# PEER on one Trainium2 core: 192 of 512 tokens by gathered rows instead of 128, the odd 64 tokens in column halves

## The chip, the cores and the metric

The kernel runs on one core of one Trainium2 chip. The metric is the device time of one execution in microseconds (us). The program has five engines' instruction streams: PE (TensorE, matrix products), DVE (VectorE), ACT (ScalarE), POOL (GpSimd) and SP (SyncE, which here only issues transfers). Transfers from ACT, SP and POOL go through queues of their own to the core's 16 DMA engines.

## The reference, cut to what matters

The program is one layer of a trunk over 512 tokens of width 1024: two mixers, their merge, and then the PEER feed-forward part, the only one that the change touches. All of it is float32.

```python
def peer_ffn(x, w_q, sub_keys, u, v):              # 8 heads, top 16 each, 128 x 128 experts
    def block(xb):
        q = (xb @ w_q).reshape(TB, H, 2, PEER_HALF)
        s = jnp.einsum('thpc,phnc->thpn', q, sub_keys)
        s1, i1 = lax.top_k(s[:, :, 0], K)
        s2, i2 = lax.top_k(s[:, :, 1], K)
        ...
        top_s, pos = lax.top_k(cand, K)
        eidx = jnp.take_along_axis(cidx, pos, axis=-1).reshape(TB, H * K)
        g = jax.nn.softmax(top_s, axis=-1).reshape(TB, H * K)
        h = jnp.einsum('tkd,td->tk', u[eidx], xb)
        a = jax.nn.gelu(h, approximate=False) * g
        return jnp.einsum('tk,tkd->td', a, v[eidx])
    ...
x = x + peer_ffn(rmsnorm(x, norm_ffn), ...)
return rmsnorm(x, norm_final)
```

Each token picks 128 of 16384 experts; u and v hold one row of 1024 float32 an expert, 64 MiB each.

## The kernel before

**Two ways to the same sum.** The first block of 128 tokens is done *by rows*: for each of its 128 picks k, one indirect transfer on POOL's queue (`row`, L757) fetches 128 rows of 4 KB, one a token, from u or v, and one DVE instruction uses them: `u_row` (L762) multiplies by the token and sums, `v_row` (L770, L772) adds a weighted row to `acc`. That makes 256 gathers of 512 KB. The other three blocks (384 tokens) are done *densely*: u and v are read whole, in 128 chunks j of 128 experts; `u_chunk` (L739) forms all 384 x 128 products and the gelu, and `v_parts` and `v_product` (L883, L911) multiply by a matrix of weights, which is zero for experts that were not picked, and by the chunk of v.

**Products in three passes.** A float32 operand is cut into a rounded high part (ACT, type fp32r) and the rest, the low part (DVE, L110, L895, L908). `mm3` (L74) then issues three PE products, lines 77, 78 and 79. Products that PE takes in float32 itself (L148 and L652, for example) appear in the profile as two records each.

**Stages.** Four stages follow each other from 456 us on:

1. The *picks*: for each of 8 heads two `query` products of 512 columns, `scores`, three `u_chunk`s (seven in the last head), then `picks` (L670), a long run of DVE instructions that ends in `eidx` (L709), the row numbers.
2. The *weights*: 48 `u_chunk`s (j from 28 to 75), and between them the dense weight matrix G, made eight tokens at a time (`g_group`, L834, 48 groups: two DVE instructions, 16 PE products, two ACT copies) and written to memory, `g_d`, in 12 transfers of 2 MB. The gelu results of the first 76 chunks go to memory too (`h_d`).
3. *u and v together*: 52 steps, each with one `u_chunk` (j from 76 on) and one chunk of v.
4. *v alone*: the chunks of v whose gelu results lie in `h_d`, 76 in all, then the sums, the final norm and the output.

`some_rows` (L777) sets how many rows are placed at each chunk: the rates R0 to R3 for the four stages are 0, 1, 2.9 and 0.95, and none is placed at the last NOROW = 8 chunks of stage 2. `pace[0]`, the last low part on DVE, is the point behind which the rows are placed. The row buffers (`gp`, L749) are four: a gather waits until DVE has used the row four before it.

## Time and profile before

| | |
|---|---|
| median of 3 runs | 1708.71 us (1706.27 to 1711.08) |
| the profiled execution | 1711.65 us, its span 1709.9 us |
| PE busy | 1675.5 us, 98% of the span |
| PE weight loads busy | 1465.9 us, 86% |
| DVE, ACT, POOL busy | 1340.8, 729.3, 377.0 us |
| moved by DMA | 414.90 MB, 243 GB/s over the span |
| mean granted clock of TensorE | 0.996 |

Times are of one profiled execution. Busy time of PE is modelled at the ends of products, which overlap; the distance between the starts of two products tells the pace. DMA share is the mean busy share of the 16 DMA engines; it can read a little over 1.00 where packets overlap.

### The profile page before, as it was taken

The numbers are of one execution on the slowest core, as the hardware profiler recorded it, in microseconds if no ns is written. First come the engines' busy times: TensorE is split into PE (matmuls) and PEld (weight loads), VectorE is DVE, ScalarE is ACT, GpSimd is POOL, SyncE is SP. The second block draws the span as 40 slices with busy tenths as digits, with TensorE's granted clock in tenths as the row PEclk, the third lists the DMA queues.
The fourth block names the chain that finished last, engine by engine and source line by source line (L and its number), as shares of the span: only waits on it lengthen the run. The fifth ranks groups of instructions, "written<-read, shape, count | busy, mean of one in ns | idle before, by whom it ended". The sixth has DMA issues, their size and how long they took to land.

```text
span 1709.9 us, 24687 instructions
## 1 busy us (share of the span) xinstructions
PE 1675.5 (98%) x9095; PEld 1465.9 (86%) x9097; DVE 1340.8 (78%) x2573; ACT 729.3 (43%) x1052; POOL 377.0 (22%) x284
## 2 busy tenths in 40 slices
PE   8999999999999999999999999999999999999997
PEld 6988887777798888999999999999999978888886
DVE  4776887547699999998988588878887888877785
ACT  4322226734443434566666433333333333333333
POOL 2000000000010000232322144444444442333320
PEclk9999999999999999999999999999999999999999
DMA  7321233127454334798988899999999999999983
GB/s 234 131 81 50 75 125 116 56 94 241 163 177 128 126 123 131 248 359 316 359 316 336 278 338 335 337 331 319 322 317 344 324 336 353 357 333 346 321 299 131
DMA packets 172472, 414.90 MB, mean 243 GB/s; under 512 B 14744, under 2 KB 85784, under 8 KB 170688
## 3 DMA queue, kind: packets, MB, share of 16 engines
q10 hardware_dynamic: 101072, 141.70, 24.4%
q1 hardware_dynamic: 34416, 137.40, 22.6%
q0 software_dynamic: 36864, 134.23, 22.4%
q8 instruction: 71, 1.16, 0.3%
q14 instruction: 49, 0.40, 0.1%
HBM read 366.86 MB, written 49.04 MB: 243 GB/s over the span
## 4 chain that ended last, share of the span: by engine, by line
PE 41%; issue 33%; DMA 11%; POOL 9%; DVE 5%; ACT 1%; POOLq 0%; SPq 0%; ACTq 0%; DVEq 0%
POOL row L757 8%; PE acc L79 6%; PE acc L77 6%; PE acc L78 6%; DMA row<-in_peer_u,eidx 5%; PE ps_mm L77 5%; PE ps_mm L79 5%; PE ps_mm L78 5%; DMA row<-in_peer_v,eidx 4%; PE ps_hg L379 2%; PE ps_hg L77 1%; PE ps_yb L460 1%; PE ps_hg L78 1%; PE ps_hg L79 1%; DMA v_raw<-in_peer_v 1%
## 5 line engine op out<-in xcount | busy, mean ns | idle before, releaser
L108 ACT CAST w_hi<-w_raw 128x1024 fp32r<-128x1024 f32 (+2 forms) x215 | 219.2, 1020 | 401.0 <-PE ps_u L78 125.4
L110 DVE TENSOR_TENSOR w_lo<-w_raw,w_hi 128x1024 fp32r<-128x1024 f32 (+2 forms) x215 | 254.9, 1185 | 84.4 <-ACT w_hi L108 72.1
L757 POOL DMA_INDIRECT row<-in_peer_u,eidx x128 | 178.5, 1394 | 553.6 <-DVE hh L762 503.6
L77 PE MATMUL ps_u<-xfH,w_hi 128*128 128x384 f32 x800 | 274.0, 343 | 1.4 <-ACT hg L744 1.4
L78 PE MATMUL ps_u<-xfL,w_hi 128*128 128x384 f32 x800 | 270.6, 338 | 0.0
L79 PE MATMUL ps_u<-xfH,w_lo 128*128 128x384 f32 x800 | 269.9, 337 | 0.0
L757 POOL DMA_INDIRECT row<-in_peer_v,eidx x128 | 178.6, 1395 | 275.5 <-DVE acc L772 253.3
L78 PE MATMUL acc<-v_lo,aH 128*128 128x512 f32 x540 | 211.2, 391 | 3.3 <-DVE v_lo L895 3.3
L77 PE MATMUL acc<-v_hi,aH 128*128 128x512 f32 x540 | 212.1, 393 | 1.4 <-ACT aH L906 1.1
L79 PE MATMUL acc<-v_hi,aL 128*128 128x512 f32 x540 | 212.1, 393 | 0.1
L906 ACT CAST aH<-aj 128x384 fp32r<-128x384 f32 x128 | 65.6, 513 | 308.7 <-DVE aj L903 138.1
L772 DVE SCALAR_TENSOR_TENSOR acc<-row,ah,acc 128x1024 f32<-128x1024 f32 x127 | 162.6, 1281 | 21.4 <-DMA row<-in_peer_v,eidx 20.7
L762 DVE CUSTOM_DVE_ANT_0 scr<-row,xf 128x1024 f32<-128x1024 f32 x128 | 156.3, 1221 | 20.1 <-DMA row<-in_peer_u,eidx 19.3
L77 PEld LDWEIGHTS ps_u<-xfH,w_hi 128*128 128x128 f32 x800 | 150.2, 188 | 3.5 <-ACT hg L744 1.7
L78 PEld LDWEIGHTS ps_u<-xfL,w_hi 128*128 128x128 f32 x800 | 150.5, 188 | 2.2
L79 PEld LDWEIGHTS ps_u<-xfH,w_lo 128*128 128x128 f32 x800 | 150.2, 188 | 0.0
L895 DVE TENSOR_TENSOR v_lo<-v_raw,v_hi 128x1024 fp32r<-128x1024 f32 x90 | 110.0, 1223 | 24.1 <-ACT v_hi L894 23.5
L78 PEld LDWEIGHTS acc<-v_lo,aH 128*128 128x128 f32 x540 | 101.7, 188 | 24.0 <-DVE v_lo L895 3.6
L79 PEld LDWEIGHTS acc<-v_hi,aL 128*128 128x128 f32 x540 | 101.8, 188 | 23.2 <-DVE aL L908 0.8
L77 PEld LDWEIGHTS acc<-v_hi,aH 128*128 128x128 f32 x540 | 101.7, 188 | 22.1 <-ACT aH L906 1.4
L894 ACT CAST v_hi<-v_raw 128x1024 fp32r<-128x1024 f32 x90 | 94.4, 1048 | 51.6 <-PE acc L79 19.9
L858 ACT COPY stg<-ps_g 128x512 f32<-128x512 f32 x96 | 99.6, 1158 | 3.3 <-PE ps_g L855 3.3
(313 smaller groups left out, 3367.4 us busy)
## 6 DMA issues: line engine op xcount, KB each, us to landing
w_raw<-in_uT SPq DMA_DIRECT2D x128, 512.0 KB
v_raw<-in_peer_v ACTq DMA_DIRECT2D x90, 512.0 KB
g_d<-stg SPq DMA_DIRECT2D x12, 2048.0 KB
gj<-g_d ACTq DMA_DIRECT2D x32, 768.0 KB
w_raw<-in_peer_v ACTq DMA_DIRECT2D x38, 512.0 KB
w_raw<-in_wT SPq DMA_DIRECT2D x31, 512.0 KB
h_d<-hg ACTq DMA_DIRECT2D x76, 192.0 KB
hgr<-h_d ACTq DMA_DIRECT2D x76, 192.0 KB
```

The lines of the kernel that those rows point to most:

```text
L77: pe.matmul(ps, lh, rh, start=first, stop=False, **kw)
L78: pe.matmul(ps, lh, rl, start=False, stop=False, **kw)
L79: pe.matmul(ps, ll, rh, start=False, stop=last, **kw)
L108: act.copy(hi[:, :n], raw[:, :n])
L110: pace[0] = dve.tensor_tensor(lo[:, :n], raw[:, :n], hi[:, :n].bitcast(F32), op=OP.subtract)
L757: pool.indirect_dma_start(out=g, out_offset=None, in_=A[tab], in_offset=bass.IndirectOffsetOnAxis(ap=eidx[:, k:k + 1], axis=0))
L762: dve.tensor_tensor_reduce(out=scr, in0=row("peer_u", k), in1=xf0, scale=1.0, scalar=0.0, op0=OP.mult, op1=OP.add, accum_out=hh[:, k:k + 1])
L772: dve.scalar_tensor_tensor(acc, row("peer_v", k), ah[:, k:k + 1], acc, op0=OP.mult, op1=OP.add)
L858: act.copy(stg[:, :, t4:t4 + 4].rearrange("p j t -> p t j"), ps)
L894: act.copy(vh, raw)
L895: pace[0] = dve.tensor_tensor(vl, raw, vh.bitcast(F32), op=OP.subtract)
L906: act.copy(aH, gj)
```

## The change

- **Tokens.** The rows take 192 tokens. The odd 64 (the first half of block 1) share one set of 64 gathers: partitions 0 to 63 fetch the picks 0 to 63 and partitions 64 to 127 the picks 64 to 127 of the same tokens (`eidh`, `gwh`, `xfh`). So there are 64 more gathers for u and 64 more for v, 384 in all. The dense part has NT = 320 tokens: `u_chunk` products have 320 columns instead of 384, G has 40 groups and 10 transfers instead of 48 and 12, `h_d` rows are 1280 B instead of 1536 B.
- **The odd half block in v.** Dense block 1 is now 64 tokens. It meets v in float32 products with 64 columns of weights (`v_halves`), once for two chunks: the even chunk's product goes to partitions 0 to 63 of `hacc`, the odd one's to 64 to 127. At the end a product with the matrix `sel` adds the halves, of `hacc` and of the row sums.
- **Plain chunks.** Each third chunk of v (42 of 128) is multiplied in float32 (L946 of the new file), one product in place of three, and its high and low parts are not made.
- **Low parts on POOL.** In the picks, `query` and `u_chunk` make the low part with a POOL instruction instead of a DVE instruction: 16 and 28 of them.
- **Rates.** R0 to R3 are 1.4, 1, 3.4 and 1.75, NOROW is 6. `pace[0]` is `eidx` in the picks, and the weighting instruction of a plain chunk.
- Buffers: chunks of v have four raw buffers of their own; `o_sum` is dropped, the sum is formed in `x2`; `gfin` is loaded at the start of stage 3.

```diff
-    def weight(src, n=1024, q=None):
+    def weight(src, n=1024, q=None, cut=None):
...
-        pace[0] = dve.tensor_tensor(lo[:, :n], raw[:, :n], hi[:, :n].bitcast(F32), op=OP.subtract)
+        i = (cut or dve).tensor_tensor(lo[:, :n], raw[:, :n], hi[:, :n].bitcast(F32), op=OP.subtract)
+        if cut is None:
+            pace[0] = i
...
+    HT = P // 2
+    T0 = P + HT
+    NT = S - T0
-    NT = 3 * P
...
-        hi, lo = cut(weight(A["peer_wq"][m]), 8)
+        hi, lo = cut(weight(A["peer_wq"][m], cut=pool), 8)
...
-    R0, R1, R2, R3, NOROW = 0, 1, 2.9, 0.95, 8
+    R0, R1, R2, R3, NOROW = 1.4, 1, 3.4, 1.75, 6
+    PLAIN = 3
...
-            mm3(ps[:, :NT], (hi[:, c, :], lo[:, c, :]), (xfH[:, c, P:], xfL[:, c, P:]), c == 0, c == 7)
+            mm3(ps[:, :NT], (hi[:, c, :], lo[:, c, :]), (xfH[:, c, T0:], xfL[:, c, T0:]), c == 0, c == 7)
...
-    rows = list(range(P))
+    rows = [(0, k) for k in range(P)] + [(1, k) for k in range(HT)]
...
-            u_chunk(j, psum([P, 512], "hg"))
+            u_chunk(j, psum([P, 512], "hg"), pool)
...
-            some_rows(R0, h * 16)
+            some_rows(R0, h)
...
-        work = [(b, t0) for b in range(3) for t0 in range(0, P, TB)]
+        work = [(b, t0) for b in range(3) for t0 in range(0 if b else HT, P, TB)]
...
+    hacc = [vp.tile([P, 512], F32, name="hacc_%d" % n) for n in range(2)]
...
+    def v_product(b, n, part, first, last):
+        gj, raw, a, v = part
+        ns = slice(n * 512, (n + 1) * 512)
+        bs = slice(b * P, (b + 1) * P)
+        if a is None:
+            pe.matmul(accs[b][n], gj[:, HT:][:, bs], raw[:, ns], start=first, stop=last)
+        else:
+            mm3(accs[b][n], (a[0][:, bs], a[1][:, bs]), (v[0][:, ns], v[1][:, ns]), first, last)
+
+    def v_halves(pair, first, last):
+        for n in range(2):
+            for z, (gj, raw, _, _) in enumerate(pair):
+                pe.matmul(hacc[n][z * HT:(z + 1) * HT, :], gj[:, :HT], raw[:, n * 512:(n + 1) * 512], start=first, stop=last)
...
-    vrows = list(range(P))
+    vrows = [(1, k) for k in range(HT)] + [(0, k) for k in range(P)]
...
+        return v_parts(j, ahead.pop(0) if ahead else None, q % PLAIN == PLAIN - 1)
+
+    for q in range(0, P - 2, 2):
+        pair = []
+        for i in range(2):
+            part = chunk(q + i)
+            pair.append(part)
+            for b in range(2):
+                for n in range(2):
+                    v_product(b, n, part, q + i == 0, False)
+            some_rows(R2 if q < P - LEAD else R3)
+        v_halves(pair, q == 0, False)
```

The order of the instructions moves at three places.

PE in stage 4, one chunk of v. Before, the three products repeat for two halves of the width (`acc_0`, `acc_1`) and three blocks, 18 in all; the first block:

```order
L77 MATMUL acc_0_9386<-w_hi,aH 128x512
L78 MATMUL acc_0_9386<-w_lo,aH 128x512
L79 MATMUL acc_0_9386<-w_hi,aL 128x512
L77 MATMUL acc_1_9387<-w_hi,aH 128x512
L78 MATMUL acc_1_9387<-w_lo,aH 128x512
L79 MATMUL acc_1_9387<-w_hi,aL 128x512
```

Now, the column halves of a finished pair, then a plain chunk (L946), then a chunk in three passes:

```order
L953 MATMUL hacc_9317<-v_raw,aj 64x512 x2
L953 MATMUL hacc_9318<-v_raw,aj 64x512 x2
L946 MATMUL acc_0_9313<-v_raw,aj 128x512
L946 MATMUL acc_1_9314<-v_raw,aj 128x512
L946 MATMUL acc_0_9315<-v_raw,aj 128x512
L946 MATMUL acc_1_9316<-v_raw,aj 128x512
L77 MATMUL acc_0_9313<-w_hi,aH 128x512
L78 MATMUL acc_0_9313<-w_lo,aH 128x512
L79 MATMUL acc_0_9313<-w_hi,aL 128x512
```

Two blocks are left of three, and four products of 64 columns come once a pair, so that the array changes between 128 and 64 columns twice a pair.

POOL from the feed-forward norm to the end. Before, only the small norm steps and the gathers:

```order
L71 TENSOR_TENSOR rs_r<-rs_ms,half 128x4 x3
L71 TENSOR_TENSOR rs_r<-rs_ms,half 128x1 x4
L757 DMA row<-in_peer_u,eidx 128x1024 x128
L757 DMA row<-in_peer_v,eidx 128x1024 x128
L71 TENSOR_TENSOR rs_r<-rs_ms,half 128x1 x4
```

Now the low parts (L110) and the gathers (L773) stand in one line; the first heads:

```order
L110 TENSOR_TENSOR w_lo<-w_raw,w_hi 128x1024 x6
L773 DMA row<-in_peer_u,eidx 128x1024 x2
L110 TENSOR_TENSOR w_lo<-w_raw,w_hi 128x1024
L773 DMA row<-in_peer_u,eidx 128x1024 x2
L110 TENSOR_TENSOR w_lo<-w_raw,w_hi 128x1024
L773 DMA row<-in_peer_u,eidx 128x1024 x3
L110 TENSOR_TENSOR w_lo<-w_raw,w_hi 128x1024
```

39 gathers stand ahead of the last of the 44 low parts, and a low part behind a gather waits until the gather may be issued.

DVE at the end of one head's picks. Before, low parts stand between the steps:

```order
L110 TENSOR_TENSOR w_lo<-w_raw,w_hi 128x1024
L705 TENSOR_TENSOR oh<-oh 128x8x128
L705 TENSOR_TENSOR oh<-oh 128x8x64
L705 TENSOR_TENSOR oh<-oh 128x8x32
L707 TENSOR_TENSOR e_4599<-oh 128x128
L709 SCALAR_TENSOR_TENSOR eidx<-e_4599 128x16
L110 TENSOR_TENSOR w_lo<-w_raw,w_hi 128x1024
```

Now the rows' multiply-and-sum (L779, two instructions a row) stands there instead:

```order
L715 TENSOR_TENSOR oh<-oh 128x8x32
L717 TENSOR_TENSOR e_4614<-oh 128x128
L719 SCALAR_TENSOR_TENSOR eidx<-e_4614 128x2x16
L779 ISA scr,hh<-row,xf_3281 128x1024
L779 ISA hh 128x1
L670 MAX v_4817<-sc 128x8
```

Three to five of them stand behind each head's `eidx`.

## Rows read from the trace of the kernel before

**Rows 1.** The page, part 2: DMA share in tenths in 40 slices of the span, and GB/s.
```profile
DMA  7321233127454334798988899999999999999983
GB/s 234 131 81 50 75 125 116 56 94 241 163 177 128 126 123 131 248 359 316 359 316 336 278 338 335 337 331 319 322 317 344 324 336 353 357 333 346 321 299 131
```
**Rows 2.** Windows, the four stages: stretch, its length, PE, PEld, DVE, ACT, POOL busy, PEclk, DMA share, GB/s.
```profile
456.00:691.00 235.00, 227.82 (x1250) 206.53 (x1248) 218.51 (x945) 100.40 (x148) 5.58 (x7) 1.00 0.42 136
691.00:955.00 264.00, 261.05 (x1988) 252.84 (x1989) 220.85 (x238) 170.55 (x207) 71.05 (x45) 1.00 0.88 322
955.00:1380.00 425.00, 420.54 (x2110) 381.56 (x2108) 341.62 (x434) 148.08 (x204) 192.06 (x142) 1.00 0.93 325
1380.00:1697.00 317.00, 316.75 (x1368) 257.93 (x1369) 247.96 (x304) 112.33 (x158) 90.06 (x66) 0.99 0.92 319
```
**Rows 3.** The timeline of PE: a stretch of stage 4, first and last of 53 products.
```profile
1499.81 0.39 PE L79 MATMUL acc<-w_hi,aL 128*128 128x512 f32 x1
...
1511.81 0.39 PE L77 MATMUL acc<-v_hi,aH 128*128 128x512 f32 x1
```
**Rows 4.** The timeline of PE: one u chunk of stage 3, 24 products of 384 columns.
```profile
1104.93 0.34 PE L77 MATMUL ps_u<-xfH,w_hi 128*128 128x384 f32 x1
...
1109.15 0.39 PE L77 MATMUL acc<-v_hi,aH 128*128 128x512 f32 x1
```
**Rows 5.** The timeline of PE: 20 products of 256 columns in the first query.
```profile
468.82 0.28 PE L78 MATMUL ps_mm<-xfL,w_hi 128*128 128x256 f32 x1
...
471.13 1.05 PE L652 MATMUL ps_tr<-kT,qT 128*128 128x128 f32 x8
```
**Rows 6.** The timeline of PE: four float32 products of 512 columns, eight records.
```profile
12.20 4.00 PE L148 MATMUL ps_tr<-sq,ones 128*128 128x512 f32 x8 [1.24 <-ACT sq L147]
15.63 0.70 PE L77 MATMUL ps_mm<-w_hi,xnH 128*128 128x290 f32 x1
```
**Rows 7.** The timeline of PE: the 16 products of one group of G.
```profile
701.84 1.10 PE L855 MATMUL ps_g<-ow,oz 128*128 128x128 f16 x16
```
**Rows 8.** Groups by shape, DVE: line, operation, count, busy us, mean ns, idle before.
```profile
L110 DVE TENSOR_TENSOR w_lo<-w_raw,w_hi 128x1024 fp32r<-128x1024 f32 x191 | 233.1, 1220 | 80.8 <-ACT w_hi L108 68.6 <-PE ps_g L855 10.5 <-issue 1.5
L772 DVE SCALAR_TENSOR_TENSOR acc<-row,ah,acc 128x1024 f32<-128x1024 f32 x127 | 162.6, 1281 | 21.4 <-DMA row<-in_peer_v,eidx 20.7
L762 DVE CUSTOM_DVE_ANT_0 scr<-row,xf 128x1024 f32<-128x1024 f32 x128 | 156.3, 1221 | 20.1 <-DMA row<-in_peer_u,eidx 19.3
L895 DVE TENSOR_TENSOR v_lo<-v_raw,v_hi 128x1024 fp32r<-128x1024 f32 x90 | 110.0, 1223 | 24.1 <-ACT v_hi L894 23.5 <-issue 0.4
```
**Rows 9.** Windows of the gathers alone (L757), POOL busy and count by stage.
```profile
456.00:691.00 235.00, 4.49 (x5) 1.00 0.42 136
691.00:955.00 264.00, 71.05 (x45) 1.00 0.88 322
955.00:1380.00 425.00, 192.06 (x142) 1.00 0.93 325
1380.00:1697.00 317.00, 89.49 (x65) 0.99 0.92 319
```
**Rows 10.** The page, part 3: the queue of the gathers.
```profile
q0 software_dynamic: 36864, 134.23, 22.4%
```
**Rows 11.** Windows of 100, 20 and 4 us with the highest DMA rates.
```profile
1400.00:1500.00 100.00, 99.92 (x434) 81.17 (x433) 85.07 (x104) 37.95 (x52) 30.47 (x25) 1.00 1.01 356
1420.00:1440.00 20.00, 20.00 (x89) 16.31 (x88) 16.03 (x20) 7.22 (x10) 4.99 (x5) 1.00 1.06 368
824.00:828.00 4.00, 4.00 (x28) 4.00 (x26) 3.70 (x5) 2.67 (x4) 0.57 (x1) 1.00 1.09 465
```
**Rows 12.** Groups by shape: PE's first 64-row product after 128-row ones, and the next.
```profile
L77 PE MATMUL ps_hg<-akH,aqH 64*128 64x512 f32 x6 | 3.0, 494 | 0.3 <-issue 0.3
L78 PE MATMUL ps_hg<-akL,aqH 64*128 64x512 f32 x6 | 2.3, 391 | 0.0
```
**Rows 13.** Groups by shape, POOL: its only wide elementwise step.
```profile
L145 POOL TENSOR_TENSOR sq<-xt 128x512 f32<-128x512 f32 x4 | 5.3, 1324 | 8.5 <-DMA xt<-in_xT 8.4
```

More of the change, by code (lines that the diff above doesn't have):

```diff
@@ L593, in norm_ffn @@
         dve.scalar_tensor_tensor(xf, x2[:, b, :], r, gffn, op0=OP.mult, op1=OP.mult)
+        if b == 1:
+            for z in range(2):
+                act.dma_start(xfh[z * HT:(z + 1) * HT, :], xf[:HT, :])
         for c4 in range(2):
@@ L768, in v_row, with u_row @@
-    def v_row(k):
+    def u_row(half, k):
+        c = half * P + k
+        dve.tensor_tensor_reduce(out=scr, in0=row("peer_u", half, k), in1=xfh if half else xf0, scale=1.0, scalar=0.0,
+                                 op0=OP.mult, op1=OP.add, accum_out=hh[:, c:c + 1])
+        n = HT if half else P
+        if k == n - 1:
+            cs = slice(half * P, half * P + n)
+            act.activation(ah[:, cs], hh[:, cs], AF.Gelu)
+            dve.tensor_tensor(ah[:, cs], ah[:, cs], gwh if half else gw0[:, 0, :], op=OP.mult)
@@ L775, in trunk, with some_rows @@
+    rows = [(0, k) for k in range(P)] + [(1, k) for k in range(HT)]
     due = [0]
-    def some_rows(rate, avail=P):
+    def some_rows(rate, heads=9):
         due[0] += rate
@@ L946, in last_rows, with chunk @@
         finish(0)
-    for q, j in enumerate(order[:-2]):
+    def chunk(q):
+        j = order[q]
         if LEAD + AHEAD + q < P:
             ahead.append(u_chunk(LEAD + AHEAD + q, up.tile([P, 512], F32, name="ps_u")))
-        a, v = v_parts(j, ahead.pop(0) if ahead else None)
-        for b in range(3):
-            for n in range(2):
-                v_product(b, n, a, v, q == 0, False)
-        some_rows(R2 if q < P - LEAD else R3)
-        if q == P - 6:
-            last_rows()
-    if 0 not in fin:
-        last_rows()
```

177 lines of the change are left out of this document (98 added, 79 removed).

## The prediction

> **What bounds the kernel now.** I read the page's slices first, then the windows of the stages, then PE's timeline inside a stage, then the groups by shape. The slices show two halves of a program: up to slice 17 the DMA engines have room, from then on they are nine tenths busy until the last slice but one [rows 1]. The windows tell the four stages apart [rows 2]: the picks take 235 us, the weights 264, u and v together 425, v alone 317; 456 us lie ahead of them and 13 behind. PE is busy for 97 to 100% of each, at a granted clock of 0.99 to 1.00 (the 2.4 GHz level), and the timeline says that this is no artefact of modelled ends: in stage 4, 53 products of 512 columns start one behind the other in 12.00 us, 0.231 us each [rows 3], and a u chunk of 24 products of 384 columns takes 4.22 us, 0.176 each [rows 4]. A step of stage 3 is then 4.22 + 18 x 0.231 = 8.38 us by PE, and 52 of them 436 us, against the 425 of the window, which holds 51. So before the change PE's pace sets stages 3 and 4. DMA is the next limit and close: share 0.93 and 0.92 over the two stages, 325 and 319 GB/s, and in one stretch of 100 us 1.01 at 356 GB/s [rows 2, 11]. In the picks DVE is at 93% and PE at 97%; there DMA idles (0.42).
>
> That is what the change trades: PE work goes away, and DMA work comes in at the stages where DMA has 7% left.
>
> **PE's side.** The dense u products get narrower. 256 columns take 2.31 / 20 = 0.1155 us a product [rows 5], 384 take 0.176; 320 are not in the trace, the middle is 0.146. That gives back 24 x 0.030 = 0.72 us a chunk: 20 us in the picks (28 chunks), 35 in stage 2 (48), 37 in stage 3 (52). Eight groups of G fewer give 8 x 1.1 = 9 us in stage 2 [rows 7].
>
> The v products: a float32 product of 512 columns is two records; eight records start 3.43 us ahead of the next product, 0.43 each, so 0.86 us a product [rows 6]. A chunk cost 18 x 0.231 = 4.16 us. A chunk in three passes now costs 12 x 0.231 = 2.77, a plain one 4 x 0.86 = 3.44: 86 x 2.77 + 42 x 3.44 = 383 us. The column halves are four float32 products a pair, 64 pairs. No row has such a product. From above: they run one after the other, 3.44 us a pair, 220 us in all. From below: the even and the odd one run wholly side by side, 110 us. I take 138: each is two records in order, and only the second record of the one and the first of the other are in different columns, so that eight records fill five times 0.43. With 52 narrower u chunks (52 x 3.50 = 182) stages 3 and 4 need 383 + 182 + 138 = 703 us of PE (675 to 785), against 52 x 4.22 + 128 x 4.16 = 752 before, in 742 us of windows, which again hold one chunk less.
>
> Twice a pair the array goes from 128 columns to 64 or back. The nearest row is the change from 128 rows to 64: the first such product takes 494 ns where the next takes 391 [rows 12], 0.10 us, so 128 changes cost about 13 us, and PE stands at 716. The Trainium skill (TensorEngine Tiling (Array Packing), Key Properties) says that a change of tiling mode drains the engine, which speaks against this change, and that different tiles can load and multiply in parallel, which speaks for it; the row shows a cost of the first kind, and no row of this trace shows the second. By a whole drain, an estimate of one product's tail (0.39 - 0.23 us [rows 3]), the 13 us would be 20.
>
> **DMA's side.** A gather moves 0.524 MB; by its queue's row 256 of them hold 22.4% of the engines' span, 1.50 us each [rows 10]. There are 128 more. Of all gathers 5 lay in the picks, 45 in stage 2, 207 behind it [rows 9] (one is counted twice). By the new order 39 lie in the picks and 42 in stage 2, so 303 behind: 96 more, +50.3 MB. Less is read of G (10 blocks for 12, -4.2 MB) and of `h_d` (76 x 32 KiB, -2.5 MB). Stages 3 and 4 moved 425 x 325 + 317 x 319 = 239.2 MB; now 282.8. At which rate? From below 322 GB/s, what they had; from above 368, the best 20 us of stage 4 [rows 11]. I take 353, just under the 356 of the full 100 us, since there the engines were at 1.01 and PE was not held up: 282.8 / 353 = **801 us**, against PE's 716. So DMA becomes the limit of stages 3 and 4, and they go from 742 to 801 us: **+59**. PE then waits about a tenth of the time, in pieces, and its products cost nothing more.
>
> **The other engines there.** DVE gets 96 rows at 1.22 + 0.08 or 1.28 us (+124 us) and loses 42 low parts of v (-51) and some of the narrower steps [rows 8]: 590 + 60 of 801 us, less full than before. POOL issues a gather in about 1.4 us, 303 x 1.4 = 424 us: room. ACT loses 42 casts. All of it lies beside DMA.
>
> **Picks.** DVE loses 44 low parts, 53 us, and gets 34 more rows, 44 us: from 218 to 209 us busy. At the same fullness the stage takes 225 us: **-10**. PE (208) and DMA (about 50 MB in 225 us) stay below. POOL's subtraction is not in the trace; 128x512 takes 1.32 us [rows 13], 128x1024 so from 1.3 (the DVE-like bound) to 2.65. Taking 2.65, a head has 5 x 2.65 + 5 x 1.4 = 20 us on POOL in about 26: covered, as long as no gather ahead of a low part waits. If that cover is gone, `w_lo` is late and PE idles.
>
> **Weights.** PE goes from 261 to 217 us; DMA moves 85.0 - 1.6 - 4.2 - 1.6 = 77.7 MB, 220 us at 353. Both are near; I take 227 us: **-37**. If DMA and PE overlapped perfectly it would be 220, and at the old ratio of DMA share (0.88) 250.
>
> **End.** Four float32 products and two copies for the joined block: **+3** (0 to 6). The moved load of `gfin` and the dropped `o_sum`: nothing, they lie in stage 3 beside transfers that are 0.2% larger by them.
>
> Sum: 1709.9 + 59 - 10 - 37 + 3 = 1725 us of span. The profiled execution ran 1.8 us longer than its span and 2.9 us above the median of the runs shown, so the median forecast is **1724 us**, 0.9% slower. About 0.3% (5 us) is what a measurement of this kernel can tell from no change. With rates from 343 to 362 GB/s this case gives 1703 to 1747.
>
> **Rivals.** (1) *DMA is not full, and the change is faster.* It ends on the other side when stages 3 and 4 fall under 786 us, that is from 360 GB/s on. For: 4 us at 465 GB/s, and 20 us at 368 [rows 11]; nothing in stages 3 and 4 before shows an engine that waited long for a transfer. Against: those 4 us hold G's large pieces, the 20 us have a share of 1.06, and no 100 us exceed 356. At 368 the sum is 1691; if DMA drops out altogether, PE's 716 at 98% sets 730 and the sum is 1653. I take 1680. The Trainium skill (HBM Reference, Specifications (TRN2)) gives about 425 GB/s to a core that streams alone; no stretch here longer than some microseconds agrees, and by that figure, an estimate, DMA would need 665 us and PE would set the end.
>
> (2) *The column halves do not run side by side.* Then that part does not do what it says: PE needs 785 + 13 = 798 us in stages 3 and 4, as much as DMA, and two full engines that wait for each other's buffers lose more; before, PE at 99% lived beside DMA at 0.93. At 0.96 of the larger one the stages take 832 and the sum is 1755. For: float32 products are two records that run in order [rows 6]. Against: the pair writes different partitions of one bank.
>
> (3) *A gather holds up low parts on POOL.* The fifth gather of a head waits until DVE has used a row, behind a run of picks; low parts queue behind it and PE with them. At 4 us a head, 8 heads, the picks give +22 in place of -10: 1756. For: low parts stand right behind groups of three gathers in the new order. Against: 4.2 rows a head and four buffers, so mostly rows of the head before.
>
> **How the numbers follow.** Main case 0.48, rival (1) 0.28, (2) 0.18, (3) 0.06. Faster by over 0.3% (under 1704): all of (1) and a sixth of the main case, 0.36. Within 0.3%: a quarter of the main case, 0.12. Slower: 0.52. The range leaves out the far half of (1), the case without any DMA limit, and the far ends of (2) and (3): 1672 to 1762.
>
> **What would show it.** DMA share at 0.97 to 1.0 through stages 3 and 4 at about 353 GB/s; PE's starts no longer even there, with waits for casts that wait for transfers; stage 2 near 227 us, the picks near 225. The halves' records show the pair: starts 0.43 us apart all along mean no overlap. I am wrong if stages 3 and 4 together take less than 780 us or if PE is still back to back in them; if the rate is above 365 GB/s, rival (1) holds; if POOL waits for DVE in front of low parts and the picks exceed 240 us, rival (3).

## The result, and the profile after

The changed kernel takes 1849.8 us (median of 4 runs, 1845.18 to 1850.37) against 1709.89 (4 runs, 1706.27 to 1713.85): the ratio is 1.081, with a 95% interval from 1.078 to 1.084. It is 8.1% slower; the forecast was 0.9%. The profiled execution took 1849.76 us, its span 1848.0.

The windows of the changed kernel's stages, with the forecast's own marks (about 10 us before the first product of v, 12 behind the last of u; columns as in [rows 2]), the end in the last row:

```profile
456.00:719.00 263.00, 221.87 (x1257) 198.69 (x1255) 236.61 (x957) 97.26 (x147) 162.32 (x85) 0.96 0.58 189
719.00:948.00 229.00, 221.99 (x1869) 215.19 (x1869) 205.09 (x235) 151.28 (x193) 67.21 (x43) 1.00 0.92 339
948.00:1427.00 479.00, 410.41 (x1927) 306.56 (x1925) 338.07 (x459) 113.57 (x169) 218.37 (x173) 0.94 0.87 313
1427.00:1832.00 405.00, 341.11 (x1124) 184.57 (x1125) 275.76 (x323) 76.02 (x111) 152.43 (x131) 0.92 0.93 330
1832.00:1848.00 16.00, 6.47 (x22) 3.65 (x20) 8.86 (x20) 5.94 (x15) 1.63 (x3) 0.78 0.27 99
```

| | before [rows 2] | forecast | after | off by |
|---|---|---|---|---|
| picks | 235 | 225 | 263 | +38 |
| weights | 264 | 227 | 229 | +2 |
| u and v together, v alone | 742 | 801 | 884 | +83 |
| end | 13 | 16 | 16 | 0 |
| span | 1709.9 | 1725 | 1848 | +123 |

The bytes of the two v stages came as reckoned (0.479 x 313 + 0.405 x 330 = 283.6 MB; forecast 282.8), the rate did not: 321 GB/s in place of 353. And no engine is full there: PE is busy for 86 and 84%, DMA for 87 and 93%. The page's slices, which answer to [rows 1], show the holes, and a granted clock that falls from stage 3 on:

```profile
PEclk9999999999999999999999998998999889898999
DMA  7322242066464657999989988897987899999995
GB/s 241 114 69 65 72 137 87 30 206 227 133 232 158 202 176 237 363 359 358 360 319 377 325 314 312 288 326 270 332 307 265 308 339 353 330 341 332 361 324 206
```

While the DMA engines are busy they are as fast as forecast. The DMA view of 400 us inside stage 3 (1000 to 1400), by queue, each with its bytes in MB and its share of the 16 engines' time:

```profile
DMA packets 46367, 124.32 MB, mean 311 GB/s; under 512 B 3744, under 2 KB 17824, under 8 KB 46346
q0 software_dynamic: 20531, 74.76, 51.9%
q10 hardware_dynamic: 20055, 28.31, 20.0%
q1 hardware_dynamic: 5760, 20.97, 14.7%
```

The shares sum to 0.87, and 124.32 MB in 0.87 x 400 us are 357 GB/s. The Trainium skill (SBUF — State Buffer, A bandwidth-pool intuition that's wrong) gives about 358 GB/s between HBM and a core. The 357 lies beside it, but the runs do not bear it out as a limit: the engines of run 16 below moved 386 GB/s for 100 us at the start of its stage 3 (share 1.02). The 425 that the prediction quoted from another page of the Trainium skill was not reached over 20 us in any run; run 16 from 1017 to 1037 has 408.

```profile
957.00:1057.00 100.00, 97.64 (x481) 71.80 (x482) 87.01 (x138) 25.48 (x39) 56.15 (x46) 1.00 1.02 386
```

So the first question for stages 3 and 4 is not how fast a transfer is, but why the engines stand idle for an eighth of their time in stage 3.

PE's timeline in stage 4 (where [rows 3] had one product each 0.23 us) shows a pair's column halves, and what a wait costs beyond itself:

```profile
1601.13 3.59 PE L946 MATMUL acc<-v_raw,aj 128*128 128x512 f32 x8
1604.66 1.94 PE L953 MATMUL hacc<-v_raw,aj 128*64 128x512 f32 x8
1609.38 0.79 PE L77 MATMUL acc<-v_hi,aH 128*128 128x512 f32 x1 [2.79 <-ACT v_hi L921]
...
1611.66 0.63 PE L77 MATMUL acc<-v_hi,aH 128*128 128x512 f32 x1
1612.09 0.63 PE L78 MATMUL acc<-v_lo,aH 128*128 128x512 f32 x1
...
1616.08 0.39 PE L79 MATMUL acc<-w_hi,aL 128*128 128x512 f32 x1
1616.31 0.40 PE L77 MATMUL acc<-w_hi,aH 128*128 128x512 f32 x1
1618.51 1.94 PE L953 MATMUL hacc<-v_raw,aj 128*64 128x512 f32 x8
1620.38 3.70 PE L946 MATMUL acc<-v_raw,aj 128*128 128x512 f32 x8
```

Four half products take 1.87 us (1618.51 to 1620.38), 0.47 each, where a full-width float32 product takes 0.88 ((1604.66 - 1601.13) / 4). The eight records of a pair, shown merged here, start in twos, 0.01 us apart, so the two halves do run side by side; 1.87 us is the median over the pairs. After PE had stood 2.79 us for a cast, its products start 0.43 us apart, the pace of the lower level (1.2 GHz), until about 1615.5; then 0.23 again.

The first seven waits of stage 3 (958 to 1415; total us, times, longest): ACT stands in front of its cast until a raw v has landed, and POOL until DVE has freed a row buffer. PE's own longest wait is for DVE's low part of u, and DVE in turn stands for ACT's cast of v.

```profile
ACT v_hi L921 <- DMA v_raw<-in_peer_v: 154.5, 22, 16.2
POOL row L773 <- DVE hh L779: 147.7, 85, 13.0
ACT aH L936 <- DVE aj L930: 126.6, 27, 10.8
POOL row L773 <- DVE acc L795: 72.8, 37, 10.3
PEld ps_u L79 <- DVE w_lo L110: 49.7, 20, 7.7
PE ps_u L79 <- DVE w_lo L110: 44.5, 19, 7.5
DVE v_lo L922 <- ACT v_hi L921: 42.2, 10, 9.2
```

A long wait is not by itself a cost: run 11 below has 203.9 us of the first one in stage 3 and is 46 us shorter there.

In the picks DVE's own instructions have grown. Groups by shape of the changed kernel's picks, DVE and POOL; outside the picks the row instruction (L779) takes 1221 ns as in [rows 8]:

```profile
L779 DVE CUSTOM_DVE_ANT_0 scr<-row,xf 128x1024 f32<-128x1024 f32 x35 | 55.2, 1577 | 11.4 <-DMA row<-in_peer_u,eidx 11.1
L713 DVE TENSOR_TENSOR oh<-oh,fi 128x2048 f16<-128x2048 f16 x7 | 12.6, 1803 | 0.7
L711 DVE TENSOR_TENSOR oh<-abf,io16k 128x2048 f16<-128x2048 f16 x8 | 11.9, 1484 | 0.3
L110 POOL TENSOR_TENSOR w_lo<-w_raw,w_hi 128x1024 fp32r<-128x1024 f32 x44 | 111.1, 2527 | 80.0 <-ACT w_hi L108 76.6 <-DMA w_raw<-in_uT 3.0
```

### The profile page after: what moved, and what is told of

Same layout as the page of the kernel before. It is cut to its first block, busy times and chain, and to the rows that moved or that the text cites. A ratio compares the mean times of both kernels' runs of the same rounds, so it can differ in the third digit from the quotient of the medians.

```text
span 1848.0 us, 23871 instructions
## 1 busy us (share of the span) xinstructions
PE 1645.8 (89%) x8553; PEld 1270.8 (69%) x8553; DVE 1364.9 (74%) x2625; ACT 634.5 (34%) x955; POOL 617.3 (33%) x457
## 4 chain that ended last, share of the span: by engine, by line
PE 34%; DMA 27%; issue 20%; POOL 9%; DVE 8%; ACT 2%; ACTq 0%; POOLq 0%; SPq 0%; DVEq 0%
DMA v_raw<-in_peer_v 9%; POOL row L773 7%; PE ps_mm L77 5%; PE ps_mm L79 5%; PE ps_mm L78 5%; DMA row<-in_peer_v,eidh 5%; DMA row<-in_peer_u,eidh 4%; DMA row<-in_peer_u,eidx 4%; DMA row<-in_peer_v,eidx 3%; PE ps_hg L79 2%; POOL w_lo L110 2%; PE ps_hg L77 2%; PE ps_hg L78 2%; PE ps_hg L381 2%; DVE scr L779 1%
## 5 line engine op out<-in xcount | busy, mean ns | idle before, releaser
L79 PE MATMUL ps_u<-xfH,w_lo 128*128 128x320 f32 x800 | 257.6, 322 | 46.9 <-DVE w_lo L110 46.8
L795 DVE SCALAR_TENSOR_TENSOR acc<-row,ah,acc 128x1024 f32<-128x1024 f32 x190 | 243.4, 1281 | 61.9 <-DMA row<-in_peer_v,eidh 33.0
L77 PE MATMUL ps_u<-xfH,w_hi 128*128 128x320 f32 x800 | 260.6, 326 | 4.9 <-ACT w_hi L108 4.0
L773 POOL DMA_INDIRECT row<-in_peer_u,eidx x128 | 175.9, 1375 | 261.3 <-DVE hh L779 236.6
L78 PE MATMUL ps_u<-xfL,w_hi 128*128 128x320 f32 x800 | 253.7, 317 | 0.0
L110 DVE TENSOR_TENSOR w_lo<-w_raw,w_hi 128x1024 fp32r<-128x1024 f32 (+2 forms) x171 | 201.2, 1177 | 50.3 <-ACT w_hi L108 49.1
L773 POOL DMA_INDIRECT row<-in_peer_v,eidx x128 | 149.9, 1171 | 235.4 <-DVE acc L795 216.1
L779 DVE CUSTOM_DVE_ANT_0 scr<-row,xf 128x1024 f32<-128x1024 f32 x128 | 168.7, 1318 | 35.1 <-DMA row<-in_peer_u,eidx 34.4
L946 PE MATMUL acc<-v_raw,aj 128*128 128x512 f32 x336 | 153.4, 599 | 5.7 <-DMA v_raw<-in_peer_v 4.0
L77 PE MATMUL acc<-v_hi,aH 128*128 128x512 f32 x244 | 111.1, 455 | 51.9 <-ACT v_hi L921 36.6
L921 ACT CAST v_hi<-v_raw 128x1024 fp32r<-128x1024 f32 x61 | 63.8, 1046 | 253.5 <-DMA v_raw<-in_peer_v 247.3
L110 POOL TENSOR_TENSOR w_lo<-w_raw,w_hi 128x1024 fp32r<-128x1024 f32 x44 | 111.1, 2527 | 80.0 <-ACT w_hi L108 76.6
L953 PE MATMUL hacc<-v_raw,aj 128*64 128x512 f32 x512 | 125.6, 606 | 1.8 <-DVE aj L930 1.8
L78 PE MATMUL acc<-v_lo,aH 128*128 128x512 f32 x244 | 110.7, 454 | 13.7 <-DVE v_lo L922 13.6
L946 PEld LDWEIGHTS acc<-v_raw,aj 128*128 128x128 f32 x336 | 63.3, 193 | 78.8 <-issue 72.9
L773 POOL DMA_INDIRECT row<-in_peer_u,eidh x64 | 82.4, 1288 | 104.0 <-DVE hh L779 97.7
```

Of the source, the lines that this page charges most:

```text
L77: pe.matmul(ps, lh, rh, start=first, stop=False, **kw)
L78: pe.matmul(ps, lh, rl, start=False, stop=False, **kw)
L79: pe.matmul(ps, ll, rh, start=False, stop=last, **kw)
L110: i = (cut or dve).tensor_tensor(lo[:, :n], raw[:, :n], hi[:, :n].bitcast(F32), op=OP.subtract)
L773: pool.indirect_dma_start(out=g, out_offset=None, in_=A[tab], in_offset=bass.IndirectOffsetOnAxis(ap=ap, axis=0))
L779: dve.tensor_tensor_reduce(out=scr, in0=row("peer_u", half, k), in1=xfh if half else xf0, scale=1.0, scalar=0.0, op0=OP.mult, op1=OP.add, ...
```

## The experiments

Each is an edit of the changed kernel. The table has all of them by one set of marks (first `ps_u` product, first half product, last `ps_u` product, and 14 to 16 us ahead of the span's end), by which the changed kernel's v stages are 457 + 417 = 874 us. With the forecast's marks, which lie 10 us ahead and 12 behind, the same are 479 + 405 = 884. The stages are those of one profiled execution; runs 5 to 12 and 14 have one time each. Stage 3 of runs 2, 3, 4 and 14, whose edits leave it as it is, lies between 460 and 467 us (457 in the changed kernel), and stage 4 of runs 3 and 14 at 412 and 409 (417), so differences of 10 us in one stage say nothing.

| run | picks | weights | stage 3 | stage 4 | whole |
|---|---|---|---|---|---|
| changed kernel | 263 | 239 | 457 | 417 | 1849.8 |
| 1 six row buffers | 265 | 241 | 468 | 414 | 1861.2 |
| 2 seven raw buffers in stage 4 | 269 | 238 | 462 | 409 | 1845.8 |
| 3 low parts on DVE | 260 | 251 | 463 | 412 | 1859.7 |
| 4 no rows in the picks | 229 | 237 | 467 | 443 | 1846.7 |
| 5 a quarter of the gathered bytes | 262 | 235 | 365 | 329 | 1663.2 |
| 6 short row instructions | 247 | 229 | 460 | 422 | 1829.8 |
| 7 run 1, v_raw of stage 4 on SP | 265 | 245 | 463 | 384 | 1829.9 |
| 8 no half products | 264 | 240 | 393 | 407 | 1776.5 |
| 9 half products 16 columns wide | 263 | 242 | 409 | 398 | 1784.0 |
| 10 half products that hold no v_raw | 266 | 242 | 408 | 391 | 1779.3 |
| 11 run 1, all v_raw on SP | 261 | 240 | 411 | 382 | 1767.3 |
| 12 all v_raw on SP, four row buffers | 264 | 242 | 431 | 384 | 1793.2 |
| 13 run 11, hgr and gj on SP too | 265 | 238 | 442 | 415 | 1834.3 |
| 14 POOL's low parts 128 wide | 238 | 238 | 460 | 409 | 1818.6 |
| 15 run 11, low parts on DVE, half the rows in the picks | 246 | 250 | 410 | 403 | 1778.2 |
| 16 run 11 again, 4 runs | 262 | 239 | 408 | 383 | 1766.3 |

### Buffers (runs 1 and 2)

```diff
-    gp = ctx.enter_context(tc.tile_pool(name="gp", reuse_waits="tile", bufs=4))
+    gp = ctx.enter_context(tc.tile_pool(name="gp", reuse_waits="tile", bufs=6))
...
-            fin[b] = [vs.tile([P, 2, 512], F32, name="o_fin", bufs=3), vs.tile([P, 2], F32, name="ss")]
+            fin[b] = [vs.tile([P, 2, 512], F32, name="o_fin", bufs=1), vs.tile([P, 2], F32, name="ss")]
```

> Edit: six buffers for the gathered rows in place of four (paid for by one o_fin buffer in place of three); the same bytes and the same work. Two theories for the 83 us that stages 3 and 4 (u and v together, v alone: 948 to 1832 us of the changed kernel's profile) took above the forecast. RATE theory: the DMA engines cannot carry the mix of gathers and streams faster than the 321 GB/s that was measured; then stages 3 and 4 stay at 884 us within 10 and the whole at 1850 within 10. CHAIN theory: the DMA engines stand idle at times because a transfer is issued only when a buffer is freed by an engine that itself waits in order behind another transfer; then two more row buffers let the gathers start earlier, and the two stages take 20 to 60 us less, the whole 1790 to 1830.

```diff
-        raw = vt.tile([P, D], F32, name="v_raw", bufs=4)
+        if j < LEAD and j % 2:
+            raw = wst.tile([P, WN], F32, name="w_raw", bufs=3)[:, :D]
+        else:
+            raw = vt.tile([P, D], F32, name="v_raw", bufs=4)
```

> Edit: in the last stage (v alone, 1427 to 1832 us) every odd chunk's raw v goes into the three weight buffers, which stand unused there, besides the four v_raw buffers: seven buffers instead of four, same bytes. RATE theory: the stage stays at 405 us within 6. CHAIN theory (ACT stands 247 us in front of its v_hi casts waiting for a v_raw that was issued too late): the stage shortens by 15 to 40 us, the whole to 1810 to 1835.

Run 1 came out as the rate theory had it in the two stages, 882 us by the table, with the whole 1 us outside its bounds. Run 2's stage 4 fell by 8 us, which is more than the 6 of the rate theory, less than the 15 of the chain theory, and no more than untouched runs differ. (The 247 us of its expectation are ACT's wait over the whole program; in stage 4 it is 84.3 us in front of `v_hi` and 48.9 in front of `w_hi`.) Six row buffers all but removed DVE's wait for rows in stage 3 (85 us to 9) without making the stage shorter: it took 468 us, and ACT's wait for `v_raw` rose from 154.5 to 194.6 us. So the chain theory in its simple form, a buffer too few, falls. The rate theory falls with the 357 GB/s above and with run 4, where stage 4 carries 349.

### Whose work it is (runs 5 and 6)

```diff
-        pool.indirect_dma_start(out=g, out_offset=None, in_=A[tab],
+        pool.indirect_dma_start(out=g[:, :256], out_offset=None, in_=A[tab].rearrange("r (a b) -> (r a) b", a=4),
...
-        return g
+        return g[:, None, :256].to_broadcast([P, 4, 256])
...
```

> Edit: each gather brings 256 of the 1024 columns (from the table seen as rows of 256 columns), and DVE's two row instructions read these 256 four times over, so that they take as long as before; the outputs of the 192 gathered tokens are therefore not computed. In stages 3 and 4 the 302 gathers then carry 40 MB in place of 158, and everything else stays: issues on POOL, row instructions on DVE, order. DMA theory (the transfers' own time, with gaps that in-order waits leave between them, sets the length): stages 3 and 4 shorten from 874 us (958 to 1832) to 720 to 770, near TensorE's need of about 700 and the last waits. DVE theory (302 row instructions of 1.25 us on DVE, 380 us, stand in front of the low parts that TensorE waits for, whatever the transfers do): stages 3 and 4 stay over 830. GATHER-ISSUE theory (POOL's 1.0 to 1.7 us per gather and its fixed latency decide): stays over 830 too, and then the next run tells it from the DVE theory.

```diff
-        dve.tensor_tensor_reduce(out=scr, in0=row("peer_u", half, k), in1=xfh if half else xf0, ...
+        dve.tensor_tensor_reduce(out=scr[:, :64], in0=row("peer_u", half, k)[:, :64], in1=(xfh if half else xf0)[:, :64], ...
...
-            dve.scalar_tensor_tensor(acc[half], row("peer_v", half, k), s, acc[half], op0=OP.mult, op1=OP.add)
+            dve.scalar_tensor_tensor(acc[half][:, :64], row("peer_v", half, k)[:, :64], s, acc[half][:, :64], ...
```

> Edit: the gathers bring all their bytes, but DVE's two row instructions work on 64 of the 1024 columns (so the outputs of the 192 gathered tokens are not computed); DVE's work in stages 3 and 4 falls by some 300 us, and a row buffer is freed about 1.1 us sooner. DMA theory: stages 3 and 4 stay within 25 us of 874, since the same 283 MB are moved. DVE theory: they shorten by 60 us or more. In the picks the row instruction (35 times 1.58 us) all but goes: there both theories expect 25 to 45 us less than 263, by DVE's busy time of 237 less about 50 and PE's 222.

Stages 3 and 4 of run 5, then of run 6 (columns as in [rows 2]):

```profile
953.00:1318.00 365.00, 363.10 (x1838) 272.95 (x1839) 320.57 (x444) 106.74 (x160) 223.11 (x165) 1.00 0.64 215
1318.00:1647.00 329.00, 322.50 (x1162) 176.02 (x1162) 283.53 (x333) 77.78 (x115) 166.52 (x138) 0.99 0.77 253
```
```profile
932.00:1392.00 460.00, 394.78 (x1843) 290.90 (x1844) 161.75 (x443) 105.98 (x160) 182.04 (x166) 0.92 0.87 314
1392.00:1814.00 422.00, 348.51 (x1158) 187.50 (x1157) 154.19 (x333) 79.15 (x116) 140.95 (x136) 0.93 0.90 322
```

With a quarter of the bytes, all of DVE's row work and all of POOL's issues, the two stages take 694 us, a little under what was expected, and PE is full at the upper clock. With all bytes and 290 us less of DVE they take 882. It is the transfers, and neither DVE nor POOL. (In the picks run 6 gained 16 us, where 25 to 45 were expected: its row instruction still takes 0.42 us, and POOL's subtractions stay.)

### What leaves the DMA engines idle (runs 7 to 13)

The changed kernel's ACT timeline in stage 3 (L921 casts a raw v, L912 issues a load of one):

```profile
1194.32 1.39 ACTq L912 DMA_DIRECT2D v_raw<-in_peer_v  x2
...
1196.10 1.04 ACT L108 CAST w_hi<-w_raw 128x1024 fp32r<-128x1024 f32 x1
1207.03 1.04 ACT L921 CAST v_hi<-v_raw 128x1024 fp32r<-128x1024 f32 x1 [9.89 <-DMA v_raw<-in_peer_v]
1207.22 0.82 ACTq L912 DMA_DIRECT2D v_raw<-in_peer_v  x2
```

Two loads are issued, ACT then stands 9.89 us in front of the cast that waits for the landing of such a load, and the next two loads stand behind that cast, although PE was done with the pair before at 1202.3. A step later the half products end at 1223.3, and ACT, which stands in front of a cast that waits for DVE, issues the next two loads only at 1232.76. The hole is not in the wait itself, in which transfers that were issued before fill the engines, but behind it (DMA share 1.01, then 0.58):

```profile
1197.00:1207.00 10.00, 6.75 (x30) 4.32 (x30) 4.01 (x6) 0.14 (x1) 2.62 (x3) 0.96 1.01 377
1222.00:1226.00 4.00, 1.97 (x11) 0.61 (x8) 4.00 (x6) 1.30 (x3) 3.05 (x2) 1.00 0.58 194
```

Runs 7, 11 and 12 take these issues off ACT:

```diff
-        act.dma_start(raw, v3[:, j, :])
+        (sync if j < LEAD else act).dma_start(raw, v3[:, j, :])
```

> Edit: six row buffers as in the first experiment, and v_raw of the last stage is issued on SP's queue in place of ACT's (where the next issue stands behind a cast that waits for the landing of the one before). If ACT's queue is what holds up the v_raw transfers of the last stage, that stage (414 us with six row buffers) shortens by 15 to 40 us, DMA share to 0.97 or more. If the bytes at the rate of busy DMA engines bind, or the buffers are freed too late by the half products, it stays within 6 us.

Runs 11 and 12 have `sync.dma_start(raw, v3[:, j, :])` in that line, for all j.

> Edit: six row buffers, and every v_raw on SP's queue, in stage 3 too (the run before this had it in stage 4 alone, where it took 30 us). If the v_raw of stage 3 come late because their issue stands behind ACT's casts, stage 3 falls from 463 to 430 or less; if they come late because their buffers are freed late, it stays within 8 us of 463, or becomes longer, since the weights of u then queue behind a v_raw that waits for its buffer.

> Edit: every v_raw on SP's queue, four row buffers as in the changed kernel. Tells whether the two more row buffers have a part in what the queue brings. If the queue alone does it, stage 4 is 380 to 390 us as with six; if the row buffers are needed as well, 395 to 417. Stage 3 as in the run before this, and 0 to 11 us shorter if six row buffers crowd out the v_raw there.

Runs 8, 9 and 10 ask what the half products have to do with it:

```diff
-        v_halves(pair, q == 0, False)
+        if q == 0:
+            v_halves(pair, True, False)
```

> Edit: the products of the odd half block with v are left out but for the first and the last pair of chunks (so half block 1 is not computed); TensorE's need in stages 3 and 4 falls by 62 pairs of 1.87 us, 116 us, and a chunk's raw v of a split chunk is freed by the low part in place of the pair's end. Transfers are the same. DMA theory: stages 3 and 4 shorten by at most 30 us from 874. TENSOR theory (TensorE's 743 busy us, with the lower clock after its waits, are the larger part of the bound, and the half products are in the way): they shorten by 70 us or more.

```diff
-                pe.matmul(hacc[n][z * HT:(z + 1) * HT, :], gj[:, :HT], raw[:, n * 512:(n + 1) * 512], start=first, stop=last)
+                w = 512 if first or last else 16
+                pe.matmul(hacc[n][z * HT:(z + 1) * HT, :w], gj[:, :HT], raw[:, n * 512:n * 512 + w], start=first, stop=last)
```

> Edit: the half products stay where they are, with all their waits, but each is 16 columns wide in place of 512 (but for the first and last pair; so half block 1 is not computed): TensorE's time for them goes, the raw v of both chunks is still held to the end of the pair. Leaving the products out took stage 3 from 457 to 392 us (DMA share 0.99) and stages 3 and 4 from 874 to 799. HOLD theory (a v_raw buffer that is freed only at the pair's end lets the next pair's loads start too late, two at once, and the casts on ACT wait for them): stage 3 stays at 445 to 465, with ACT's wait for v_raw over 100 us. TIME theory (it is TensorE's 1.87 us a pair and what its queue delays): stage 3 falls to 390 to 410 and ACT's wait for v_raw there goes.

```diff
-                ... gj[:, :HT], raw[:, n * 512:(n + 1) * 512], start=first, stop=last)
+                ... gj[:, :HT], x2[:, 3, n * 512:(n + 1) * 512], start=first, stop=last)
```

> Edit, the opposite one: the half products keep their full width and place, but read a tile that is always there (x2) in place of the two v_raw (so half block 1 is not computed); TensorE's time stays, a split chunk's raw v is freed by its low part. HOLD theory: stage 3 falls to 390 to 415 us, DMA share 0.96 or more. TIME theory: it stays at 445 to 465.

Stage 3 of runs 9 and 10, then stages 3 and 4 of run 11, then of run 12:

```profile
961.00:1370.00 409.00, 356.40 (x1841) 283.99 (x1840) 316.71 (x439) 105.86 (x159) 212.99 (x163) 0.93 0.96 349
```
```profile
964.00:1372.00 408.00, 376.88 (x1839) 282.38 (x1838) 323.66 (x445) 107.97 (x161) 224.89 (x167) 0.97 0.97 357
```
```profile
957.00:1368.00 411.00, 379.88 (x1843) 286.75 (x1844) 326.05 (x449) 107.07 (x161) 210.45 (x168) 0.95 0.95 353
1368.00:1750.00 382.00, 338.14 (x1158) 183.17 (x1157) 281.07 (x328) 78.09 (x115) 157.05 (x133) 0.95 0.97 352
```
```profile
962.00:1393.00 431.00, 386.56 (x1843) 291.45 (x1842) 321.17 (x443) 106.38 (x160) 213.34 (x166) 0.95 0.92 334
1393.00:1777.00 384.00, 340.89 (x1157) 182.13 (x1156) 287.55 (x332) 77.88 (x115) 165.82 (x137) 0.95 0.97 356
```

With every `v_raw` on SP's queue and four row buffers stages 3 and 4 fall from 874 to 815 us; with six row buffers as well to 793, at 353 and 352 GB/s. The two more buffers, which had brought nothing while ACT issued the loads, are worth 20 in stage 3 now; run 12's expectation had them bring nothing there, or cost up to 11. Stage 4 falls by 33 us by the queue alone (30 from run 1 to run 7); seven raw buffers (run 2) had brought 8. That a free buffer is of no use to an issue that stands behind a cast would explain this; it is argued. ACT still waits for raw v, longer than before (203.9 us in stage 3 of run 11), but no load of v stands behind it.

Run 8 takes 74 us off the two stages, more than the 30 of the DMA theory and what the tensor theory asked for: the half products have a part in it. But runs 9 and 10 answer neither hold nor time alone: each of the two opposite cuts takes stage 3 from 457 to 409 or 408, while ACT's wait for `v_raw` there stays in the one (109.4 us) and goes in the other (2.8). Run 11 cuts neither and gets 411. What fits all of these is a loop that was just too long: landing, cast, low part, the products of the pair, the release at its end, the next issue on ACT; 2 us of products, an earlier release or an earlier issue each take it below the time that the DMA engines need. That each of the three suffices is measured; that it is this loop, and that the queue acts by the order of issue and not by which queue carries the load, is argued from the timeline.

```diff
-            act.dma_start(hgt, h_d[j])
+            sync.dma_start(hgt, h_d[j])
...
-            act.dma_start(gq_t[0], g_d[...])
+            sync.dma_start(gq_t[0], g_d[...])
```

> Edit: six row buffers, and every load of the v stages (v_raw, hgr, gj) on SP's queue, none on ACT's. The version before it took 1767 us with v_raw alone moved. If hgr and gj on ACT still hold up transfers, stages 3 and 4 fall from 793 to 770 to 785 us (357 GB/s, the rate of busy DMA engines, would give 783); if the DMA engines are full as it is (shares 0.95 and 0.97), the whole stays at 1767 within 6; if a gj that waits for its buffer now stands ahead of v_raw and the weights, it becomes longer by 5 to 20. Against the kernel before (1710) it stays slower by 2.5 to 3.5 per cent, since 283.6 MB at 357 GB/s alone need 794 less what is outside, where the kernel before needed 742.

This was a miss: 1834.3 us, ratio to the kernel before 1.072 (1.067 to 1.077), 67 us slower than run 11 instead of 20 at most. SP's waits in stages 3 and 4 of this run (959 to 1816): L925 is the load of `hgr` from `h_d`, whose buffer DVE frees, and behind it stand the loads of u (L106) and v (L912).

```profile
SPq L106 <- DVE w_lo L110: 241.5, 34, 17.8
SPq L925 <- DVE aj L930: 209.4, 67, 10.2
SPq L912 <- PE hacc L953: 117.8, 41, 7.4
```

By these waits it is the same fault as on ACT, made anew on SP: an issue that waits for its buffer holds up others. That is argued; the two loads that were moved were not tried apart.

### The picks (runs 3, 4, 14 and 15)

Run 3: `cut=pool` becomes `cut=None` in `query`, and `u_chunk` is called without `pool`; the low parts then set `pace[0]` again, so the rows stand behind them and not behind `eidx`. Run 4: R0 = 0 and R3 = 2.25.

> Edit: the low parts of the picks stage go back to DVE, the gathers of the picks (1.4 a chunk) stay. CONTENTION theory (POOL's 2.5 us subtractions slow DVE's own instructions, which take 1.58 and 1.73 us instead of 1.22): the u row products and the f16 compares fall back to 1.22 us, DVE's busy time is about 239 + 53 - 12 - 10 = 270 us, and that is the length: picks 265 to 280 us, no shorter than the 265 measured. ORDER theory (DVE has room, but POOL's queue delivers low parts late because gathers waiting for a free row buffer stand ahead of them): without POOL in the way picks falls to 235 to 250 us. If the instructions of DVE stay at 1.58 and 1.73 us, it is the gathers' work on POOL or the rows landing, not the subtractions, that slows them.

> Edit: no gathers in the picks (rate 0 instead of 1.4 a chunk; the last stage's rate 2.25 instead of 1.75 takes them), the low parts stay on POOL. CONTENTION theory: the f16 compares on DVE stay near 1.7 us, since POOL's subtractions go on, and picks falls only by the row products, to about 215 to 230 us. ORDER theory (gathers ahead of low parts on POOL's queue hold them up): picks falls to about 205 to 220 us and PE's wait for low parts (30 to 34 us) all but goes. In both, stages 3 and 4 take up 39 more rows (20 MB, 57 to 62 us at 321 to 353 GB/s), so that the whole comes out between 1845 and 1870 if the DMA engines bound them.

```diff
-        i = (cut or dve).tensor_tensor(lo[:, :n], raw[:, :n], hi[:, :n].bitcast(F32), op=OP.subtract)
+        m = n if cut is None else P
+        i = (cut or dve).tensor_tensor(lo[:, :m], raw[:, :m], hi[:, :m].bitcast(F32), op=OP.subtract)
...
+        if w[1].shape[1] == P:
+            return w[0].rearrange("p (c m) -> p c m", c=c), w[1][:, None, :].to_broadcast([P, c, P])
```

> Edit of the changed kernel: in the picks POOL's low part is 128 columns in place of 1024, and TensorE reads these 128 for all eight products of the third pass, so that every product, wait and gather stays (the low parts, and with them every output that hangs on the picks, are wrong). CONTENTION theory: DVE's row instruction and compares go from 1.58 and 1.73 back to 1.22 us, DVE's busy time in the picks from 237 to about 190, and the stage from 263 to 222 to 235. LATE theory (the gathers ahead on POOL's queue, and not the subtraction, make the low parts late): DVE's instructions return to 1.22 too, but TensorE still waits 20 us or more for low parts and the stage stays over 240. If DVE's instructions stay slow, the gathers or the landing rows slow them, not the subtractions.

The groups by shape of the picks of run 3 and of run 14 (its lines stand three lower); POOL's subtraction is gone in the one and 562 ns long in the other:

```profile
L779 DVE CUSTOM_DVE_ANT_0 scr<-row,xf 128x1024 f32<-128x1024 f32 x35 | 42.6, 1217 | 3.1 <-DMA row<-in_peer_u,eidx 3.1
L713 DVE TENSOR_TENSOR oh<-oh,fi 128x2048 f16<-128x2048 f16 x7 | 8.5, 1219 | 0.1
```
```profile
L782 DVE CUSTOM_DVE_ANT_0 scr<-row,xf 128x1024 f32<-128x1024 f32 x35 | 43.4, 1240 | 13.6 <-DMA row<-in_peer_u,eidx 13.3
L716 DVE TENSOR_TENSOR oh<-oh,fi 128x2048 f16<-128x2048 f16 x7 | 8.6, 1236 | 0.7
```

In both (run 3 with DVE busy for 242 us, not the 270 of its expectation, and so 260 us long), DVE's instructions are back at 1.22 to 1.24 us, with the gathers in place. Run 4, which has the subtractions without the gathers, keeps the compares at 1.73 us (L713) and 2.27 (L711). So it is POOL's subtraction. How it acts, the row instruction's spread in the picks of the changed kernel shows (min/median/max ns):

```profile
L779 DVE CUSTOM_DVE_ANT_0 scr<-row,xf x35: 1200/1224/3842, 505.1 to 703.1; 128x1024 f32<-128x1024 f32 x35
```

Most take 1.22 us, and the longest takes one subtraction more (3.84 - 1.22 = 2.6 us; POOL's take 2.35 to 3.48). Six take over 2.8 us, and each of the six ends 1.08 us after a subtraction of POOL's has ended: DVE is not slowed evenly, it stands until POOL is done. DVE is busy for 236.6 us in the picks of the changed kernel and for 208.8 in run 14, so the 44 subtractions, which had been taken off DVE at 53 us, cost it 28 again. The Trainium skill (SBUF — State Buffer, SBUF: two separate sides) states that DVE and GpSimd lock a shared pair of ports for a whole instruction, against DVE instructions with two inputs from SBUF; this trace agrees, also in the exceptions: `max` with one input takes 0.28 us inside a subtraction as outside one, and two instructions with one input from PSUM (L627, at 456.68 and 458.07) take 692 ns each while a subtraction runs from 456.40 to 458.81, against 680 to 692 in run 3.

The picks of run 14 take 238 us: 25 of the 38 us go with the subtraction. Run 14 does not part the two ways in which they may: the 28 us that DVE loses, and a POOL that is busy with subtractions for 86 us less, so that low parts come earlier (PE's wait for them falls from 35 to 12 us). The contention theory had expected 222 to 235 with DVE busy for 190; the late theory had asked for 20 us of that wait. Run 4, without the gathers and their rows, has 229 and 9 us of the wait, with the subtractions in place. Why the rest of run 14, 13 us above the 225, remains was not tried further; DVE stands 13 us for rows there. Its totals: run 3 wins 3 us in the picks and run 4 takes 34 off, and both are lost behind them (run 4 carries 39 rows more in the v stages, 910 us in place of 874).

> Edit: six row buffers, v_raw on SP's queue, the low parts of the picks on DVE again, and half as many rows in the picks (0.7 a chunk; 2.0 in place of 1.75 in the last stage). DVE's work in the picks is then 188 + 54 - 42.6 x 19/35 ... about 222 us and TensorE's 222: the picks fall from 261 to 230 to 240, and 19 rows of 0.524 MB more at 353 GB/s cost 28 us later: the whole 1755 to 1775, no better than 1767 by more than 12. If it comes below 1750, the picks bought their rows too dear.

1778.2 us, 11 above run 11 and 3 outside the expectation: the picks came to 246, not 230 to 240, and the 19 rows moved to stage 4 cost 21 us there (403 for 382). What the picks give, the v stages take.

### The best version

> The same kernel as the run with six row buffers and all v_raw on SP's queue, taken again with rounds. If the reckoning holds: 1767 within 6 us, 3.0 to 3.7 per cent above the kernel before, stages 3 and 4 at 793 within 8 us and 350 to 355 GB/s. If the one time was chance, it lies nearer to the 1793 of the version with four row buffers.

1766.3 us (1762.26 to 1774.91), 1.034 times the kernel before (1.029 to 1.039). It gives back 83 us of the 140 and is not faster than the kernel before. By rows, an estimate: weights and v stages move 77.7 + 283.6 = 361 MB; at 357 GB/s that is 1012 us, and with 456 ahead, 225 for the picks and 16 at the end 1709 us. At that rate a pipeline without holes around this change would come out where the kernel before is. But the 357 is the rate of one stretch of the changed kernel and not a limit: at the 386 of run 16's 100 us the same sum gives 1632 us. What a better order of issue could reach stays open.

## Why the prediction was wrong, step by step

- **What bounds the kernel**: right in kind. DMA takes PE's place as the limit; without most of the gathered bytes PE is full again (run 5). The forecast had 282.8 MB and 39, 42 and 303 gathers by stage; the trace has 283.6 MB and the same counts (with [rows 9], one counted twice).
- **"I take 353, just under the 356 of the full 100 us, since there the engines were at 1.01 and PE was not held up."** This is the step that failed, for 83 of the 123 us. The rate of busy engines was right (357). That they would be busy was taken from a stretch of [rows 11] in which PE was busy for 99.92 of 100 us, so that no load came too late for it. Nothing in the forecast asked who issues a load, and what stands ahead of it. With the issue moved and six row buffers the stages take 803 us by the forecast's marks (947 to 1750), at 353 and 352 GB/s by the others: the forecast's 801. That it meets this so closely is in part luck, since the engines there are idle for 5 and 3% and faster while they are busy (353 / 0.95 = 372 GB/s). The queue alone, with four row buffers, gives back 59 of the 83 us. In the kernel before, the loads stood on ACT's queue as well, but ACT waited only twice for a raw v in stages 3 and 4, 10.1 us in all. That PE's pace left DMA 7% of room [rows 2], so that a late issue cost nothing, is argued, not tried.
- **"PE then waits about a tenth of the time, in pieces, and its products cost nothing more."** It waits a seventh, and the products after a wait run at the lower level: 0.43 in place of 0.23 us, granted clock 0.94 and 0.92.
- **Picks: "At the same fullness the stage takes 225 us: -10."** Failed, +38. DVE's work was costed at the durations of [rows 8] as if POOL's subtraction lay beside it; it locks DVE out. DVE without that is busy 208.8 us (run 14), the 209 of the forecast. PE's wait for low parts, taken as covered, was 35 us. The duration of the subtraction itself, 2.65 taken, was 2.53.
- **Weights 227 and end +3**: 229 and +3.
- **Column halves**: 138 us taken, between 110 and 220. They run wholly side by side: 64 x 1.87 = 120 us, with the changes of the array inside. The lower bound was right, the argument for 5/8 wrong. The 320-column u product was taken at 0.146 us; 23 of them start one behind the other in 3.41 us of stage 3 (1194.15 to 1197.56), 0.148 each.
- **Rivals.** (1), a DMA that is not full, was wrong in sign: not full, because starved. (2) is refuted as named; its remark that two nearly full engines lose to each other's buffers is what happened, with DMA and the release of `v_raw`. (3) had its condition, picks over 240, and POOL did stand 17 us in front of gathers for DVE; but shortening the subtraction with the gathers in place brings back 25 of the 38 us (run 14), so the larger part has another reason than the one it names.
